# A new order for the output stage of the mixers: joined squares, groups C, D, A, B, pooled products between the rows

## The chip, the cores and the metric

The kernel runs on one core of a Trainium2 chip. The metric is the device time of one execution in microseconds. Five engines work side by side, each through its own list of instructions in its written order, and wait for each other by semaphores: TensorE (PE, its weight loads PEld), VectorE (DVE), ScalarE (ACT), GpSimd (POOL) and SyncE (SP), which issues the DMAs here.

## The reference

Two layers of a decoder trunk run over 320 tokens (256 of a prompt, 8 sequences of 8 samples) with 1024 channels, all in float32. Per layer:

```
x = LN(alpha*x + 0.5*(1+g1) * SwiGLU1(mod1(x)))
proj = mod2(x) @ W_in          -> u, v, xb, gate_b, gate_c, h, glu_a, glu_g
A = gelu(u) * (W_s (lower triangle, 4 heads of 64 channels) @ LN(gelu(v)) + b_s)
B = ((windowed mean of xb, windows 2/4/8/16) - xb) @ pool_w * pool_scale
C = gate_b * conv3(gate_c * h)
D = swish(LN(conv31(glu_a * sigmoid(glu_g)) + b))
x = LN(alpha*x + (1+g2) * (RMSnorm of each of A, B, C, D, 256 channels each) @ W_out)
x = LN(alpha*x + 0.5*(1+g3) * SwiGLU2(mod3(x)))
```

`mod(x) = x*(1+scale) + shift`, where scale, shift and the gates g are products of a conditioning vector with a matrix `w_ada` of 1024 x 9216 per layer. The last rows of the inputs of A, B, C and D are outputs too.

## The kernel before

Activations lie with 128 channels on the partitions and 320 tokens along the row, so 1024 channels are eight tiles and each group A to D is two. A weight tile is 128x128. For precision each weight unit (eight tiles, 128x1024) is split on the chip into a rounded high part (`whi`, a cast on ScalarE) and a low part (`wlo`, a subtraction on VectorE, L240), and each activation likewise; a product is then three matmuls of 320 columns.

All engines follow the order in which the program is written (`manual_schedule`); nothing is reordered. A class `Stream` loads raw weights through SyncE's queue six buffers ahead and splits one unit each time TensorE begins a new one (`next_unit`, called from `tile`): the cast and the subtraction stand in the lists of ScalarE and VectorE at that place. `ada_mm` puts in halves of the modulation product; each is four matmuls, one for each quarter of the 128 columns. When a part is done, `ada_step` takes it on by one stage at a time: a copy on ScalarE (`adev`, L485), a selection on TensorE (L489), an addition on VectorE (L498).

The mixers of a layer (`mix_body`) begin with ten windows of projections, during which VectorE works off 60 taps of D's convolution (L923). What then happens is written out by hand in `MIX_SEQ`, a list of words that `mix_body` performs one after the other:

- `mean`: the rest of the taps, then D's mean over 256 channels, two float32 matmuls with a constant matrix (L1116). `sub` takes it off.
- `sq g`, `stat g`, `pow g`, `bc g`, for a group g (4 is D's LayerNorm, 0 to 3 are the RMS norms of A to D): two squares on ScalarE (L834); their sum over the channels by matmuls with the squares as weights, for three blocks of tokens and both tiles (L541); a small addition on VectorE and a power on GpSimd (L1131, L1132); the broadcast over partitions by matmul (L611).
- `mul`, `hi`, `lo g`: the scaled product on VectorE (L842), its cast on ScalarE (L853), its low part on VectorE (L859).
- `vgain`, `sgu`, `sgate`: the gain of v, the spatial products of A (L1035, L1037), bias and gate on VectorE (L1046 to L1049).
- `pool0`, `pool1`: windowed sums of B's two tiles on VectorE (L958 to L969); `poolmm`: their two products on TensorE (L974), evicted on ScalarE (L977).
- `ko k`: the k-th of six rows of output products: for one of the first six input tiles, products into five accumulators (`kouter`, L681 to L686). `WO_GROUPS` says which group these tiles are of.

Behind the list comes the tail: a weight split, the next modulation's three products on VectorE, then the eight output tiles one by one (`WO_ORDER`) with the last two input tiles, each evicted (`evac`, L824 to L827), squared and added up for the next normalization, whose sums TensorE takes as `nbm` (L541).

Of the kernel before, what the change touches and what calls it, by code (L numbers as in the profile page):

```python
# [12 lines left out]
P = 128  # L13
# [52 lines left out]
WO_GROUPS = (2, 1, 3, 0)  # L66
# [4 lines left out]
    pool0 hc0 xb1 up0 val vstat up1 gc0 gb0 vnorm cconv0 gc1 hc1 gb1 mean cconv1 sub sq4 ada6 ctaps0 ctaps1 cgate0  # L71
    cgate1 stat4 pow4 vgain ada2 sq2 bc4 norm swish stat2 sq3 sgu pow2 pool1 ada2 stat3 bc2 pow3 poolmm mul2 hi2
    sq1 sgate bc3 lo2 sq0 ada2 stat1 mul3 hi3 pow1 ko0 stat0 lo3 pow0 bc1 mul1 ko1 hi1 lo1 step step bc0 mul0 hi0
    ada18 ko2 lo0 ko3 ko4 ko5
# [217 lines left out]
def sam(ap):  # L292
    return ap.rearrange("p (b t) -> p b t", t=NT_S)


class Kern:
# [568 lines left out]
    def mix_body(self, l, gb, G, late):  # L865
# [81 lines left out]
        def pool(j):  # L947
            e, es = eB[j], eBs[j]
            o = Y(f"pl{l}{j}")
            pl.append(o)  # L950
            sp = [mp.tile([P, 271], F32, tag="sp", bufs=2, name=f"s{i}p{l}{j}") for i in range(2)]
            ss = [mp.tile([P, NB, 23], F32, tag="ss", bufs=2, name=f"s{i}s{l}{j}") for i in range(2)]
            cp, cs_, sh = e, es, 1
            for g in range(2 * j + 2):
                np_, nss = sp[g % 2], ss[g % 2]
                lo = sh * 2 - 1
                p0 = 0 if g < 2 * j + 1 else 64
                V.tensor_tensor(np_[p0:P, lo:271], cp[p0:P, lo:271], cp[p0:P, lo - sh:271 - sh], op=ALU.add)  # L958
                V.tensor_tensor(nss[p0:P, :, lo:23], cs_[p0:P, :, lo:23], cs_[p0:P, :, lo - sh:23 - sh], op=ALU.add)
                if g // 2 == j:  # L960
                    q = slice(64 * (g % 2), 64 * (g % 2) + 64)
                    V.tensor_tensor(o[q, 0:16], np_[q, 15:31], self.inv[q, j, 0:16], op=ALU.mult)
                    V.scalar_tensor_tensor(o[q, 16:NP_], np_[q, 31:271], self.inv[q, j, 16:17], e[q, 31:271],
                                           op0=ALU.mult, op1=ALU.subtract)
                    V.scalar_tensor_tensor(sam(o[q, NP_:N]), nss[q, :, 15:23], self.inv[q, j, 16:17],
                                           es[q, :, 15:23], op0=ALU.mult, op1=ALU.subtract)
                cp, cs_ = np_, nss
                sh *= 2
            V.tensor_tensor(o[:, 0:16], o[:, 0:16], e[:, 15:31], op=ALU.subtract)  # L969

        def pool_mm():
            for jj in range(2):
                pb = self.mm(f"pb{l}{jj}")
# [54 lines left out]
        def spatial():  # L1028
            for jj in range(2):
                pt = self.mm(f"pm{l}{jj}")  # L1030
                for hh in range(2):
                    h = 2 * jj + hh
                    o = pt[64 * hh:64 * hh + 64]
                    for cc in range(2):
                        nc.tensor.matmul(o[:, cc * P:(cc + 1) * P], vb[cc][:, h * 64:(h + 1) * 64],  # L1035
                                         self.wsT[:, h, :], start=True, stop=True)
                    nc.tensor.matmul(o[:, NP_:N], vb[2][64:128, h * 64:(h + 1) * 64],  # L1037
                                     self.wsS[64:128, h, :], start=True, stop=True)
# [72 lines left out]
        def mean(_):  # L1111
# [3 lines left out]
            for j in range(2):  # L1115
                nc.tensor.matmul(rr[5][:, 0:N], self.o256, aD[j], start=(j == 0), stop=(j == 1))  # L1116
# [5 lines left out]
        def sq(grp):  # L1122
            qs[grp] = self.rms_sq(f"{l}{grp}", ys[grp])

# [45 lines left out]
        def taps_(n):  # L1170
            for _ in range(min(n, len(taps))):
# [6 lines left out]
               "norm": norm, "swish": swish, "ctaps": ctaps, "cgate": cgate, "vgain": lambda _: v_gain(),  # L1178
# [251 lines left out]
```

## Time and profile before

| | us |
|---|---|
| median of 3 runs | 1285.9 (1285.89 to 1292.28) |
| the profiled execution, its own time | 1289.18 |
| its span, first to last instruction | 1287.4 |
| output stage of layer 0, mean to last row | 350.96 to 387.68 |
| output stage of layer 1, mean to last row | 975.46 to 1013.66 |

The profile is one execution. Times in it count from its first instruction, and 1.8 us of the execution lie around the span. The stages are short against the whole, 36.7 and 38.2 us of 1287.4, and each holds some 280 matmuls of many kinds. Layer 0 and layer 1 run the same code; they differ in how many pieces of the modulation lie between the projections.

### The profile page before, as it was taken

How to read it: one execution, taken by the hardware profiler on the slowest of the kernel's cores; microseconds unless marked ns; L12 is line 12 of the kernel's file. 1: busy time of each engine (PE TensorE's matmuls, PEld its weight loads, DVE VectorE, ACT ScalarE, POOL GpSimd, SP SyncE). 2: the span in 40 equal slices, each digit the busy share in tenths (PEclk: the TensorE clock that was granted, in tenths of full speed). 3: DMA queues.
4: the chain of work that ended last, by engine and by line, in shares of the span. 5: the costliest groups of instructions: out<-in, count | busy, mean ns of one | idle time of the engine just before them, and what ended most of it. 6: DMA issues, size and time to landing. Idle time of an engine off the chain costs nothing.

```text
span 1287.4 us, 22297 instructions
## 1 busy us (share of the span) xinstructions
PE 1263.3 (98%) x9414; PEld 1213.7 (94%) x9414; DVE 730.0 (57%) x1321; ACT 555.8 (43%) x872; POOL 22.4 (2%) x39
## 2 busy tenths in 40 slices
PE   9999999999999999999999999999997999999996
PEld 8999999999888999999999999999995989999996
DVE  5644444468977644453575454445798775454444
ACT  3643333347444643343445343333653455343332
POOL 0000000000010000000000000000000000000000
PEclk9999999999999999999999999999998989999999
DMA  9865556568849854534465555454775694434301
GB/s 376 315 233 211 196 198 255 198 213 240 303 182 94 327 180 148 211 135 162 164 216 209 173 187 201 176 201 171 222 256 197 104 236 164 155 140 164 131 1 41
DMA packets 63748, 247.46 MB, mean 192 GB/s; under 512 B 31072, under 2 KB 33632, under 8 KB 34464
## 3 DMA queue, kind: packets, MB, share of 16 engines
q1 hardware_dynamic: 58912, 245.11, 56.9%
q8 instruction: 74, 1.21, 0.4%
q10 hardware_dynamic: 4736, 0.93, 0.4%
q14 instruction: 26, 0.21, 0.0%
HBM read 243.45 MB, written 2.57 MB: 191 GB/s over the span
## 4 chain that ended last, share of the span: by engine, by line
PE 90%; DVE 6%; ACT 2%; DMA 1%; issue 1%; POOL 0%; ACTq 0%; another core or an unknown queue 0%; SPq 0%; DVEq 0%
PE of L672 4%; PE adp L466 4%; PE oh L673 4%; PE of L673 4%; PE oh L674 4%; PE of L674 4%; PE oh L672 4%; PE uf L672 4%; PE uh L674 4%; PE uh L672 4%; PE uf L673 4%; PE uf L674 4%; PE uh L673 4%; PE gf L672 4%; PE gh L672 3%; PE gh L674 3%
## 5 line engine op out<-in xcount | busy, mean ns | idle before, releaser
L240 DVE TENSOR_TENSOR wlo<-raw,whi 128x1024 fp32r<-128x1024 f32 x312 | 373.1, 1223 | 137.3 <-ACT whi L232 136.4
L232 ACT CAST whi<-raw 128x1024 fp32r<-128x1024 f32 x312 | 315.3, 1045 | 24.4 <-issue 8.4
L672 PE MATMUL of<-hhf,whi 128*128 128x320 f32 x352 | 109.4, 311 | 0.0
L674 PE MATMUL of<-hhf,wlo 128*128 128x320 f32 x352 | 108.9, 310 | 0.0
L673 PE MATMUL of<-hlf,whi 128*128 128x320 f32 x352 | 108.9, 309 | 0.0
L672 PE MATMUL oh<-hhh,whi 128*128 128x320 f32 x352 | 108.5, 308 | 0.0
L674 PE MATMUL oh<-hhh,wlo 128*128 128x320 f32 x352 | 108.5, 308 | 0.0
L673 PE MATMUL oh<-hlh,whi 128*128 128x320 f32 x352 | 108.5, 308 | 0.0
L672 PE MATMUL uf<-xhif,whi 128*128 128x320 f32 x320 | 99.3, 310 | 0.0
L672 PE MATMUL uh<-xhih,whi 128*128 128x320 f32 x320 | 98.9, 309 | 0.0
L674 PE MATMUL uf<-xhif,wlo 128*128 128x320 f32 x320 | 98.8, 309 | 0.0
L673 PE MATMUL uf<-xlof,whi 128*128 128x320 f32 x320 | 98.8, 309 | 0.0
L673 PE MATMUL uh<-xloh,whi 128*128 128x320 f32 x320 | 98.8, 309 | 0.0
L674 PE MATMUL uh<-xhih,wlo 128*128 128x320 f32 x320 | 98.8, 309 | 0.0
L672 PE MATMUL gf<-xhif,whi 128*128 128x320 f32 x304 | 94.5, 311 | 0.0
L672 PE MATMUL gh<-xhih,whi 128*128 128x320 f32 x304 | 94.1, 309 | 0.0
L674 PE MATMUL gf<-xhif,wlo 128*128 128x320 f32 x304 | 93.9, 309 | 0.0
L673 PE MATMUL gf<-xlof,whi 128*128 128x320 f32 x304 | 93.9, 309 | 0.0
L674 PE MATMUL gh<-xhih,wlo 128*128 128x320 f32 x304 | 93.9, 309 | 0.0
L673 PE MATMUL gh<-xloh,whi 128*128 128x320 f32 x304 | 93.8, 309 | 0.0
L775 ACT CAST hhh<-sgh 128x320 fp32r<-128x320 f32 x44 | 20.2, 459 | 134.3 <-DVE sgh L772 133.8
L775 ACT CAST hhf<-sgf 128x320 fp32r<-128x320 f32 x44 | 20.2, 459 | 134.3 <-DVE sgf L772 134.3
(334 smaller groups left out, 2806.5 us busy)
## 6 DMA issues: line engine op xcount, KB each, us to landing
raw<-in_w_main SPq DMA_DIRECT2D x156, 1024.0 KB, 5.0
raw<-in_w_ada SPq DMA_DIRECT2D x72, 1024.0 KB, 6.8
out_yT<-x SPq DMA_DIRECT2D x8, 160.0 KB, 1.8
xt<-in_x SPq DMA_DIRECT2D x2, 512.0 KB, 4.2
wsT<-in_wsT SPq DMA_DIRECT2D x2, 256.0 KB
sgln<-in_sgln SPq DMA_DIRECT2D x2, 256.0 KB, 5.1
cD<-in_pre_d SPq DMA_DIRECT2D x4, 120.0 KB, 8.4
out_o_ds<-cD ACTq DMA_DIRECT2D x4, 120.0 KB, 9.7
```

The lines of the kernel that those rows point to most:

```text
L232: kk.nc.scalar.copy(hi, raw)
L240: self.kk.nc.vector.tensor_tensor(lo, raw, hi, op=ALU.subtract)
L466: nc.tensor.matmul(ps[32 * g:32 * g + 32, 0:w], self.cs[:, k, :], wt[:, h, g * w:(g + 1) * w], start=(k == 0), stop=(k == NK - 1))
L672: mm(ps, hi, xh, start=first, stop=False)
L673: mm(ps, hi, xl, start=False, stop=False)
L674: mm(ps, lo, xh, start=False, stop=last)
L775: nc.scalar.copy(hi, sg)
```

## The change

It rewrites the list, the order of the groups and four of the steps:

- `mean` adds D's two tiles on VectorE first and does one matmul instead of two. A new step `qa g` adds the two squares of a group on VectorE, so that `stat g` has three matmuls instead of six.
- The groups enter the output products in the order C, D, A, B (before: C, B, D, A). The weights of W_out are laid out in that order.
- C's broadcast stands ahead of D's group statistic, the spatial gate ahead of C's products, and C's power ahead of the spatial products.
- The 15 VectorE instructions of `pool1` are given out in three portions (`p4`, `p4`, `p9`) ahead of D's sum of squares, behind the first row of output products and behind the second; `poolmm` comes behind the third row, its second accumulator in the other PSUM tag.
- The spatial products alternate between two heads, which write to partitions 0 to 63 and 64 to 127.
- Three `step` words take the place of later `ada` words, which had nothing left to multiply and only called `ada_step`.

```diff
-WO_GROUPS = (2, 1, 3, 0)
+WO_GROUPS = (2, 3, 0, 1)
 MIX_SEQ = """
-    pool0 hc0 xb1 up0 val vstat up1 gc0 gb0 vnorm cconv0 gc1 hc1 gb1 mean cconv1 sub sq4 ada6 ctaps0 ctaps1 cgate0
-    cgate1 stat4 pow4 vgain ada2 sq2 bc4 norm swish stat2 sq3 sgu pow2 pool1 ada2 stat3 bc2 pow3 poolmm mul2 hi2
-    sq1 sgate bc3 lo2 sq0 ada2 stat1 mul3 hi3 pow1 ko0 stat0 lo3 pow0 bc1 mul1 ko1 hi1 lo1 step step bc0 mul0 hi0
-    ada18 ko2 lo0 ko3 ko4 ko5
+    pool0 hc0 xb1 up0 val vstat up1 gc0 gb0 vnorm cconv0 gc1 hc1 gb1 mean cconv1 sub sq4 ada6 ctaps0 qa4 ctaps1 cgate0
+    cgate1 stat4 pow4 vgain ada2 sq2 bc4 qa2 norm swish stat2 sq3 pow2 sgu p4 qa3 bc2 stat3 sgate sq0 mul2 hi2 pow3 step
+    qa0 step stat0 pow0 lo2 step bc3 mul3 hi3 ko0 p4 lo3 bc0 mul0 hi0 ko1 p9 lo0 ko2 poolmm ko3 sq1 qa1 stat1 pow1 ko4
+    bc1 mul1 hi1 ko5 lo1
 """.split()
...
-        def pool(j):
+        def pool_steps(j):
...
-                V.tensor_tensor(np_[p0:P, lo:271], cp[p0:P, lo:271], cp[p0:P, lo - sh:271 - sh], op=ALU.add)
+                yield V.tensor_tensor(np_[p0:P, lo:271], cp[p0:P, lo:271], cp[p0:P, lo - sh:271 - sh], op=ALU.add)
...
+        def pool_part(n):
+            if not pool1:
+                pool1.append(pool_steps(1))
+            for _ in range(n):
+                next(pool1[0], None)
 
         def pool_mm():
             for jj in range(2):
-                pb = self.mm(f"pb{l}{jj}")
+                pb = (self.rn if jj else self.mm)(f"pb{l}{jj}")[:, 0:N]
...
-                for hh in range(2):
-                    h = 2 * jj + hh
-                    o = pt[64 * hh:64 * hh + 64]
-                    for cc in range(2):
+                hs = [(2 * jj + hh, pt[64 * hh:64 * hh + 64]) for hh in range(2)]
+                for cc in range(2):
+                    for h, o in hs:
                         nc.tensor.matmul(o[:, cc * P:(cc + 1) * P], vb[cc][:, h * 64:(h + 1) * 64],
                                          self.wsT[:, h, :], start=True, stop=True)
+                for h, o in hs:
                     nc.tensor.matmul(o[:, NP_:N], vb[2][64:128, h * 64:(h + 1) * 64],
...
-            for j in range(2):
-                nc.tensor.matmul(rr[5][:, 0:N], self.o256, aD[j], start=(j == 0), stop=(j == 1))
+            s = mp.tile([P, N], F32, tag="rsq", bufs=4, name=f"sD{l}")
+            V.tensor_tensor(s, aD[0], aD[1], op=ALU.add)
+            nc.tensor.matmul(rr[5][:, 0:N], self.o256, s, start=True, stop=True)
...
+        def qa(grp):
+            a, b = qs[grp]
+            V.tensor_tensor(a, a, b, op=ALU.add)
+            qs[grp] = [a]
```

## Rows read from the trace of the kernel before

**Rows 1.** The page, part 1: busy time, share of the span, instructions per engine.
```profile
PE 1263.3 (98%) x9414; PEld 1213.7 (94%) x9414; DVE 730.0 (57%) x1321; ACT 555.8 (43%) x872; POOL 22.4 (2%) x39
```
**Rows 2.** Busy time by stretch: stage and tail of layer 0, before and in layer 1's.
```profile
core 0: us, PE busy (x) PEld busy (x) DVE busy (x) ACT busy (x) POOL busy (x), PEclk, DMA share, GB/s
350.96:387.68 36.72, 35.35 (x282) 31.23 (x281) 27.27 (x71) 17.23 (x32) 4.48 (x5) 0.95 0.49 183
387.68:405.92 18.24, 16.55 (x129) 15.54 (x127) 13.66 (x36) 8.54 (x18) 0.00 (x0) 1.00 1.04 105
969.60:975.46 5.86, 0.12 (x2) 0.00 (x1) 5.86 (x13) 0.42 (x1) 0.00 (x0) 0.93 0.43 158
975.46:1013.66 38.20, 36.83 (x280) 30.86 (x281) 27.40 (x71) 16.85 (x31) 4.48 (x5) 0.92 0.42 150
```
**Rows 3.** What TensorE waited for in the whole span: total us, times, longest us.
```profile
PE cmn L1116 <- DVE aD L923: 5.7, 1, 5.7
PE nbm L541 <- DVE Sm L583: 3.4, 2, 1.7
PE rr L541 <- ACT sqrm L834: 2.2, 2, 1.1
```
**Rows 4.** Instructions in order of time, layer 0, TensorE: start us, duration us, what.
```profile
350.96 1.24 PE L1116 MATMUL cmn<-aD,o 128*128 128x320 f32 x4
352.13 2.80 PE L466 MATMUL adp<-raw,cs 128*32 128x256 f32 x48
...
357.70 0.88 PE L611 MATMUL rr<-ident,rv 128*128 128x128 f32 x6 [0.29 <-POOL rv L1132]
358.41 1.50 PE L541 MATMUL rr<-o,sqrm 128*128 128x64 f32 x12
359.85 0.65 PE L1035 MATMUL pm<-wsT,v 128*64 128x128 f32 x4
...
363.19 0.64 PE L489 MATMUL adp<-sel,adev 128*128 128x36 f32 x4
```
**Rows 5.** The same for VectorE, layer 0.
```profile
349.93 1.22 DVE L240 TENSOR_TENSOR wlo<-raw,whi 128x1024 fp32r<-128x1024 f32 x1
...
355.40 0.89 DVE L1091 TENSOR_TENSOR yC<-yC,gbs 128x320 f32<-128x320 f32 x2
...
360.03 0.43 DVE L958 TENSOR_TENSOR s0p<-eb 128x270 f32<-128x270 f32 x1
...
363.78 0.17 DVE L969 TENSOR_TENSOR pl<-pl,eb 128x16 f32<-128x16 f32 x1
...
366.89 0.42 DVE L1046 TENSOR_TENSOR yA<-pm,sgb 128x256 f32<-128x256 f32 x1
...
368.87 0.89 DVE L859 TENSOR_TENSOR ml<-yC,mh 128x320 fp32r<-128x320 f32 x2
...
369.82 1.00 DVE L842 SCALAR_TENSOR_TENSOR aD<-aD,par,rr 128x320 f32<-128x320 f32 x2
...
372.29 1.23 DVE L240 TENSOR_TENSOR wlo<-raw,whi 128x1024 fp32r<-128x1024 f32 x1 [1.40 <-ACT whi L232]
```
**Rows 6.** The same for ScalarE, layer 0.
```profile
361.03 0.35 ACT L485 COPY adev<-adp 128x256 f32<-128x256 f32 x1
...
371.21 1.99 ACT L232 CAST whi<-raw 128x1024 fp32r<-128x1024 f32 x2
```
**Rows 7.** The same for TensorE, layer 1.
```profile
975.46 2.50 PE L1116 MATMUL cmn<-aD,o 128*128 128x320 f32 x4 [5.74 <-DVE aD L923]
977.89 4.54 PE L466 MATMUL adp<-raw,cs 128*32 128x256 f32 x48
...
997.70 0.40 PE L681 MATMUL wo<-mh,whi 128*128 128x320 f32 x1
...
999.98 1.45 PE L541 MATMUL rr<-o,sqrm 128*128 128x64 f32 x12
```
**Rows 8.** VectorE at the first eviction of the tail, layer 0.
```profile
388.76 0.23 DVE L824 TENSOR_TENSOR evsm<-wo,ada 128x64 f32<-128x64 f32 x1 [0.36 <-PE wo L674]
```

More of the change, by code (lines that the diff above doesn't have):

```diff
@@ L957, in pool @@
                 p0 = 0 if g < 2 * j + 1 else 64
-                V.tensor_tensor(np_[p0:P, lo:271], cp[p0:P, lo:271], cp[p0:P, lo - sh:271 - sh], op=ALU.add)
-                V.tensor_tensor(nss[p0:P, :, lo:23], cs_[p0:P, :, lo:23], cs_[p0:P, :, lo - sh:23 - sh], op=ALU.add)
+                yield V.tensor_tensor(np_[p0:P, lo:271], cp[p0:P, lo:271], cp[p0:P, lo - sh:271 - sh], op=ALU.add)
+                yield V.tensor_tensor(nss[p0:P, :, lo:23], cs_[p0:P, :, lo:23], cs_[p0:P, :, lo - sh:23 - sh], op=ALU.add)
                 if g // 2 == j:
                     q = slice(64 * (g % 2), 64 * (g % 2) + 64)
[L962 to L966, printed above, removed]
+                    yield V.tensor_tensor(o[q, 0:16], np_[q, 15:31], self.inv[q, j, 0:16], op=ALU.mult)
+                    yield V.scalar_tensor_tensor(o[q, 16:NP_], np_[q, 31:271], self.inv[q, j, 16:17], e[q, 31:271],
+                                                 op0=ALU.mult, op1=ALU.subtract)
+                    yield V.scalar_tensor_tensor(sam(o[q, NP_:N]), nss[q, :, 15:23], self.inv[q, j, 16:17],
+                                                 es[q, :, 15:23], op0=ALU.mult, op1=ALU.subtract)
                 cp, cs_ = np_, nss
                 sh *= 2
-            V.tensor_tensor(o[:, 0:16], o[:, 0:16], e[:, 15:31], op=ALU.subtract)
+            yield V.tensor_tensor(o[:, 0:16], o[:, 0:16], e[:, 15:31], op=ALU.subtract)
+        def pool(j):
+            for _ in pool_steps(j):
+                pass
+        pool1 = []
+        def pool_part(n):
[3 more added lines that the diff above has]
+                next(pool1[0], None)
         def pool_mm():
             for jj in range(2):
-                pb = self.mm(f"pb{l}{jj}")
+                pb = (self.rn if jj else self.mm)(f"pb{l}{jj}")[:, 0:N]
                 nc.tensor.matmul(pb, self.pw[:, jj, :], pl[jj], start=True, stop=True)
@@ L1177, in mix_body @@
                "vnorm": lambda _: v_norm(), "cconv": cconv, "t": taps_, "mean": mean, "sub": sub, "sq": sq, "stat": stat, "pow": pw_, "bc": bc, "mul": mul, "hi": hi, "lo": lo,
-               "norm": norm, "swish": swish, "ctaps": ctaps, "cgate": cgate, "vgain": lambda _: v_gain(),
+               "norm": norm, "swish": swish, "ctaps": ctaps, "qa": qa, "p": pool_part, "cgate": cgate, "vgain": lambda _: v_gain(),
                "pool": pool, "poolmm": lambda _: pool_mm(), "sgu": lambda _: spatial(),
```

## The prediction, made before the changed kernel ran

> **What bounds the kernel now.** I read the page's busy times first, then the stretches around the two output stages, then what TensorE waited for there, then each engine's instructions in order of time. TensorE is busy 98% of the span, VectorE 57% [rows 1]: time saved on TensorE counts, unless another engine is late. In the two stretches that the change rewrites (36.7 us in layer 0, 38.2 us in layer 1) VectorE is busy 27.3 of 36.7 us, far above its share of the whole, and ScalarE 17.2 [rows 2]. TensorE's waits there are small, 1.1 us a layer for squares and 0.3 for D's power [rows 3, 4]; the large one, 5.7 us in layer 1, stands ahead of the stage, where the D taps on VectorE end after the last projection [rows 3]. In the tail behind the stage TensorE ends first and waits 1.7 us a layer for VectorE's sums [rows 3]: the evictions run as one chain over VectorE and ScalarE, so what delays the first eviction delays the layer.
>
> **Prices.** A pitch is start to next start. On TensorE: the mean 1.17 us, a statistic of 12 records 1.44 (358.41 to 359.85), a broadcast 0.71, the spatial products 3.34 (359.85 to 363.19), one sixth of the modulation run 0.46 [rows 4]; a row of output products 2.28 (997.70 to 999.98, [rows 7]). On VectorE: two 128x320 products 0.89, so 0.40 pitch and 0.49 to the end for one; two scaled products 1.00; the spatial gate 1.98 (366.89 to 368.87); the pooled products 3.8 for 15 instructions (360.03 to 363.78, and the last); a weight split 1.14 pitch [rows 5]. On ScalarE: a weight cast 1.0, the modulation copy 0.35 [rows 6]. Each engine works in its written order, so I laid the new order down engine by engine: an instruction starts when its engine is free and its last operand is there, plus 0.03 us from engine to engine (the rounded gap in rows like 371.21 and 372.29). Laid down the same way, the old order ends layer 0's tail 0.12 us late and layer 1's 0.75 us late against the trace; I take these off.
>
> **What is removed.** Ten statistics lose half their records (0.72 each, 3.6 a layer), two means lose half (0.58 each). The spatial products now alternate between the two halves of the columns. No row of before shows two halves side by side: the bounds are no gain (3.34 stays) and, by the modulation run, full overlap. There 24 products of 256 columns take 2.80 us, 0.12 each, where the four 320-column records of the mean take 1.17: four column groups overlap about four times [rows 4]. Two groups would give half, 1.67. I take 1.8, nearer to the row; no gain would cost 0.46 a layer at the end, since part of it lies beside VectorE. In all some 5.7 us of TensorE per layer go.
>
> **What is added.** Six sums on VectorE per layer, 0.40 each, 2.4 us, and each stands between ScalarE's squares (or the taps) and TensorE.
>
> **Layer 0, step by step.** Mean: taps and a weight split occupy VectorE to 351.06 [rows 5], the new sum ends 351.55, the half mean ends 352.20, as before: gain nothing. D's LayerNorm statistic ends 0.6 earlier, but its power instruction stands on VectorE behind the taps and gates of C, now 0.4 longer: its broadcast comes at 357.8, before 357.70 [rows 4], and TensorE idles 1.2. C's statistic waits for its sum, which stands ahead of D's normalization: 359.2 instead of 358.4, and D's normalization is 0.4 later. The spatial products end at 361.7, 1.5 ahead of before, then C's broadcast and D's group statistic end at 363.1. Now VectorE has, from 360.2: four pool steps 1.2, D's sum (it waits for swish and squares to 361.6) 0.4, the gate 1.98, C's products 0.92, a power, A's sum 0.4: 365.4. ScalarE can cast C only behind those products, and the modulation copy stands behind that cast; TensorE waits for it 2.65 us, to 365.7 (A's statistic would wait to 365.4 anyway). Output products of C start at 367.6, 2.6 ahead of before (370.18). But VectorE's road to the pooled products is long: D's products end 369.1; D's cast and the weight cast on ScalarE end at 370.6, while VectorE waits 1.6 for the split (1.40 before, [rows 5]); split, four pool steps, D's low parts, A's products (1.14, 1.06, 0.80, 0.92) to 374.5; A's cast and the next weight cast, again 1.6 of waiting; split to 377.2; the last seven pool steps 1.7: 378.97. TensorE is done with the first three rows and the first pooled product at 375.6 and waits 3.4 us for the second, with two rows of output products (ko3 to ko5), B's statistic and broadcast queued behind it. From there TensorE needs ko3, 1.1 of waiting for B's sum (behind eviction, weight cast and squares), ko4, the broadcast, ko5: 388.9, where before it was 387.68 [rows 2]. That is +1.2. The tail's first eviction is later still: B's low parts end 388.8, and behind them stand a weight split that waits for its cast and the three modulation products; it starts at 391.0, before 388.76 [rows 8], +2.3. The tail's chain carries it to the next normalization: 408.04 - 405.92 - 0.12 = +2.0 us.
>
> **Layer 1.** The mean starts 0.8 later (the sum behind the last tap, 976.3 for 975.46) and is half as long at the low clock, so it ends 0.4 earlier, 977.5 for 977.9 [rows 7]. VectorE is ahead here, so D's halved LayerNorm statistic counts: its broadcast is 0.8 earlier. From there the steps are those of layer 0: the replay ends at 1034.67 against 1031.90, less 0.75: +2.0.
>
> **Clock.** In the old stage the granted clock averages 0.95 in layer 0, 3.7 us at the lower of its levels (1.2 GHz), after waits of 0.3 and 1.1 us; in layer 1 it is 0.92, about 6 us, after the wait of 5.7 [rows 2 to 4]; the same modulation run then takes 4.54 us instead of 2.80 [rows 4, 7]. The new waits (1.2, 0.8, 2.65, 3.4, 1.1) are more and longer. Four us at the lower level from the second pooled product on add only 0.5 per layer, since VectorE is the later one there; another 3.5 us of it from A's statistic on bring this to 1.3. I take 1.0 per layer, bounds 0 and 2.5 (the latter if a row such as ko4 or ko5 falls in it too). The Trainium skill (TensorE: Matmul & The Clock Gate, section on psum-queue depth-cycling) speaks against this change: frequent short idles between groups of matmuls let the clock swing between its levels. By that rule the low stretches last through the stage, which is the second rival below.
>
> **What moves at no cost.** DMAs: the weight loads follow VectorE's splits, one to two us later than before, while the DMA share of the stage is 0.49 [rows 2]; without that slack a split would wait. POOL's five powers keep their number. The new order of groups only renames the weight tiles. A's statistic and B's take their accumulator from C's and A's products, which end before either is due.
>
> **Sum.** +2.0 +2.0 +2x1.0 = +6.0 on the profiled 1289.18 (span 1287.4): 1295.2. That execution lies 3.3 us above the median, 1285.9, which I take to shift alike: 1292.0, with 1288 to 1297 for this case.
>
> **Rivals.** *Pooled products in time* (faster): if VectorE reaches the last pool steps 3.4 us earlier, the wait at the second pooled product goes, the tail starts at 385.5 and each layer gains 1.4: 1285.9 - 2.8 = 1283; with every cut of TensorE effective 11.4 less, 1274.5. For it: TensorE is 98% busy. Against: VectorE's chain is made of instructions whose durations stand in the rows, and its two waits for a weight cast are there already in the old order. It decides from the point where pool's end lies before 375.6 in layer 0. *Clock low through the stage*: 4.54/2.80 is 1.6 times; with bounds of 2.5 per layer and no overlap of the spatial products (0.46) it is 1285.9 + 4.0 + 5.9 = 1296, to 1299. For it the many waits; against it that the same 1.1 us wait ahead of the first row of output products leaves that row at full clock in layer 1, 2.28 us [rows 3, 7]. *Waits and cuts cancel*: VectorE's additions hide in its old idle (9.4 us of 36.7, [rows 2]) and the stage ends as before: 1286 to 1288. For it the idle; against it that this idle is waiting on ScalarE and TensorE within the same chain.
>
> **Chances.** Forecast 0.62, pooled products in time 0.12, clock 0.14, cancel 0.12. 0.5% is 6.4 us, about what a measurement of this kernel can tell from no change. The forecast is split about evenly by that bound: slower 0.31 + 0.14 + 0.02 = 0.47, faster 0.10, the rest 0.43. Range 1281 to 1299: down over half of the faster case, up over the clock case.
>
> **What would show it.** In the changed profile: TensorE waits about 3.4 us on a pool instruction at the second pooled product and about 2.6 us at the modulation's selection, in both layers; statistics of 6 records at 0.7 pitch; spatial products 1.7 to 1.8 together; output products starting about 2.6 us earlier in the stage and their fourth row later than before. A pool end before TensorE's third row, or a stage shorter than 36.7 us, would make the forecast wrong.

## The result and the profile after

The changed kernel takes 1301.55 us (median of 6 runs, 1298.21 to 1303.57) against 1288.66 us for the kernel before, run beside it (1285.89 to 1294.05, 6 runs). The ratio is 1.0087, 95% interval [1.0065, 1.0109]: slower, as forecast, but by 11 us (by the ratio) to 13 us (by the medians) where the forecast had 6. The time lies above the range. Of the 9.5 us between it and the forecast of 1292.0, 2.8 are the base: the forecast started from 1285.9, the median of three runs, and with six runs that is 1288.66.

The profiled execution of the changed kernel took 1301.87 us, its span is 1300.1. Busy time of each engine in the span, as in [rows 1]:

```profile
PE 1262.2 (97%) x9350; PEld 1212.7 (93%) x9350; DVE 735.6 (57%) x1333; ACT 556.5 (43%) x872; POOL 27.1 (2%) x39
```
TensorE does 1.1 us less, VectorE 5.6 us more, the span (1287.4 before) is 12.7 us longer. GpSimd does as many instructions as before and is busy 4.7 us longer with them; that is the first sign of what the forecast missed. The stretches that answer to [rows 2], stage and tail of layer 0 and of layer 1:

```profile
core 0: us, PE busy (x) PEld busy (x) DVE busy (x) ACT busy (x) POOL busy (x), PEclk, DMA share, GB/s
351.68:393.30 41.62, 34.75 (x248) 30.07 (x249) 28.11 (x74) 16.69 (x31) 7.83 (x5) 0.84 0.45 173
393.30:412.62 19.32, 16.60 (x129) 15.58 (x127) 14.65 (x37) 8.97 (x19) 0.00 (x0) 0.99 0.71 74
984.10:1024.75 40.65, 34.32 (x249) 28.43 (x249) 27.95 (x74) 16.66 (x31) 5.76 (x5) 0.86 0.41 152
1024.75:1044.04 19.29, 16.56 (x129) 15.54 (x127) 14.62 (x36) 8.95 (x19) 0.00 (x0) 0.99 0.93 74
```
The stages are 41.6 and 40.7 us long, before 36.7 and 38.2 [rows 2]. TensorE is busy for less of them, its granted clock is 0.84 and 0.86 (0.95 and 0.92), and the five powers take 7.83 us of GpSimd in layer 0. What TensorE waited for in the whole span (total us, times, longest), as in [rows 3]:

```profile
PE cmn L1129 <- DVE sD L1128: 7.2, 2, 6.7
PE nbm L541 <- DVE Sm L583: 5.5, 2, 2.7
PE pb L986 <- DVE pl L969: 3.9, 2, 2.0
PE rr L611 <- POOL rv L1150: 3.5, 2, 3.2
PE adp L489 <- ACT adev L485: 3.1, 2, 2.5
PE rr L541 <- DVE sqrm L1140: 2.7, 3, 1.1
```
The forecast's waits are there: the second pooled product (`pb`), the selection (`adp`), the sums of squares. One is there that it had at 1.2 us and that is 3.2: D's broadcast in layer 0, released by GpSimd. TensorE in layer 0, in order of time:

```profile
351.68 0.81 PE L1129 MATMUL cmn<-sD,o 128*128 128x320 f32 x2 [0.49 <-DVE sD L1128]
...
360.23 0.88 PE L611 MATMUL rr<-ident,rv 128*128 128x128 f32 x6 [3.20 <-POOL rv L1150]
360.94 1.43 PE L541 MATMUL rr<-o,sqrm 128*128 128x64 f32 x6
362.30 1.12 PE L1046 MATMUL pm<-wsT,v 128*64 128x128 f32 x8
...
365.23 1.54 PE L611 MATMUL rr<-ident,rv 128*128 128x128 f32 x6
366.56 1.49 PE L541 MATMUL rr<-o,sqrm 128*128 128x64 f32 x6
368.62 1.07 PE L489 MATMUL adp<-sel,adev 128*128 128x36 f32 x4 [0.58 <-ACT adev L485]
```
The broadcast right behind the wait still takes 0.88 us, as at the full clock [rows 4]; the next one, at 365.23, takes 1.54. The granted clock is at the lower level, 1.2 GHz, from 361.0 to 374.6. GpSimd's power that TensorE waited for:

```profile
357.13 3.04 POOL L1150 TENSOR_TENSOR rv<-rv,mhalf 128x3 f32<-128x3 f32 x1 [27.03 <-DVE rv L1149]
```
and in the kernel before the same instruction, on three numbers per partition:

```profile
356.68 0.96 POOL L1132 TENSOR_TENSOR rv<-rv,mhalf 128x3 f32<-128x3 f32 x1 [26.66 <-DVE rv L1131]
```
There VectorE had waited 0.15 us ahead of the small addition that hands the power its operand:

```profile
356.44 0.16 DVE L1131 TENSOR_SCALAR rv<-rr 128x3 f32<-128x3 f32 x1 [0.15 <-PE rr L541]
```
VectorE beside it, in the changed kernel: the small addition, reached without a wait, then v's gain and C's joined squares without a gap, to 359.46.

```profile
356.90 0.15 DVE L1149 TENSOR_SCALAR rv<-rr 128x3 f32<-128x3 f32 x1
356.98 2.09 DVE L1034 TENSOR_TENSOR v<-v,sgln 128x256 f32<-128x256 f32 x6
358.98 0.48 DVE L1140 TENSOR_TENSOR sqrm<-sqrm,sqrm 128x320 f32<-128x320 f32 x1
```
The power ends 0.71 us behind that run. In layer 1 the same instructions stand beside it, but there VectorE had waited 0.82 us ahead of the small addition, and the power took 0.96 us:

```profile
990.85 0.16 DVE L1149 TENSOR_SCALAR rv<-rr 128x3 f32<-128x3 f32 x1 [0.82 <-PE rr L541]
```
So in layer 1 the forecast's steps show undisturbed (TensorE):

```profile
984.10 1.43 PE L1129 MATMUL cmn<-sD,o 128*128 128x320 f32 x2 [6.73 <-DVE sD L1128]
...
994.29 0.66 PE L1046 MATMUL pm<-wsT,v 128*64 128x128 f32 x8
...
995.99 0.88 PE L611 MATMUL rr<-ident,rv 128*128 128x128 f32 x6
996.71 0.83 PE L541 MATMUL rr<-o,sqrm 128*128 128x64 f32 x6
...
1000.02 1.07 PE L489 MATMUL adp<-sel,adev 128*128 128x36 f32 x4 [2.48 <-ACT adev L485]
```
The spatial products take 1.70 us together (994.29 to 995.99; forecast 1.7 to 1.8, before 3.34), the selection waits 2.48 (forecast 2.65), and behind that wait the clock is again low. Last, the sums of the next normalization in layer 0:

```profile
412.62 1.54 PE L541 MATMUL nbm<-o,Sm 128*128 128x64 f32 x6 [2.72 <-DVE Sm L583]
413.95 1.49 PE L541 MATMUL rbm<-o,Qm 128*128 128x64 f32 x6
415.23 1.49 PE L611 MATMUL nbm<-ident,vm 128*128 128x128 f32 x6
```
The wait is 1.0 us longer than before [rows 3], and what follows runs at 1.2 GHz; before, the first of these took 0.88.

### The profile page after: what moved, and what is told of

The parts are those of the page before. It is cut to its first block, busy times and chain, and to the rows that moved or that the text cites. A ratio compares the mean times of both kernels' runs of the same rounds, so it can differ in the third digit from the quotient of the medians.

```text
span 1300.1 us, 22179 instructions
## 1 busy us (share of the span) xinstructions
PE 1262.2 (97%) x9350; PEld 1212.7 (93%) x9350; DVE 735.6 (57%) x1333; ACT 556.5 (43%) x872; POOL 27.1 (2%) x39
## 4 chain that ended last, share of the span: by engine, by line
PE 68%; issue 19%; DVE 9%; ACT 2%; POOL 0%; POOLq 0%; ACTq 0%; DVEq 0%
PE of L672 4%; PE of L673 4%; PE of L674 4%; PE uf L672 4%; PE adp L466 4%; PE uf L674 4%; PE uf L673 4%; PE gf L672 3%; PE gf L674 3%; PE gf L673 3%; DVE wlo L240 3%; DVE aD L923 3%; PE oh L674 2%; PE oh L673 2%; PE oh L672 2%
```

## The experiments

Besides these two, seventeen kernels were run. For each, "layer 0" and "layer 1" are the time in us from the start of D's mean to the start of the normalization's sums in its profile (behind added matmuls, where there are some), the ratio is that of its runs to those of the kernel before beside it, with its interval. Where the text says that a kernel is so many us faster or slower, that is its ratio taken of 1290 us.

| kernel | ratio | layer 0 | layer 1 |
|---|---|---|---|
| before | 1 | 54.96 | 56.44 |
| changed | 1.0087 [1.0065, 1.0109] | 60.94 | 59.94 |
| inter_only | 0.9962 [0.9939, 0.9986] | 51.79 | 53.70 |
| join_only | 1.0053 [1.0033, 1.0072] | 61.38 | 56.76 |
| order_nojoin | 1.0057 [1.0034, 1.0080] | 59.46 | 59.49 |
| fill | 1.0077 [1.0050, 1.0104] | 59.00 | 59.41 |
| vgain_late | 1.0092 [1.0065, 1.0118] | 60.59 | 62.08 |
| pool_8 | 1.0046 [1.0026, 1.0066] | 60.25 | 58.11 |
| step_early | 1.0069 [1.0043, 1.0095] | 60.09 | 59.24 |
| qa4_only | 1.0074 [1.0043, 1.0106] | 61.46 | 55.33 |
| qa4_fill | 1.0051 [1.0026, 1.0076] | 55.27 | 55.12 |
| order_fill | 1.0052 [1.0033, 1.0071] | 58.49 | 59.37 |
| order_mended | 0.9992 [0.9974, 1.0011] | 53.79 | 56.48 |
| nbm_fill | 1.0080 [1.0052, 1.0107] | 61.59 | 59.69 |
| fill_all | 1.0069 [1.0044, 1.0095] | 59.16 | 59.23 |
| best3 | 0.9933 [0.9910, 0.9956] | 52.20 | 50.58 |
| best_all | 0.9934 [0.9916, 0.9953] | 51.01 | 53.61 |
| best_c | 0.9910 [0.9895, 0.9925] | 49.79 | 52.14 |
| best_c_fill | 0.9889 [0.9868, 0.9909] | 49.80 | 50.06 |

The two right columns come from one execution each, and the low clock does not last equally long in every one. The edit of *nbm_fill* stands behind layer 0's stage and tail, and yet its layer 0 is 0.65 us longer than the changed kernel's: the clock is low for 17.1 us there instead of 13.7. So a difference of about a microsecond between two rows is weak evidence.

**One part at a time.** *inter_only*: the kernel before with the alternating spatial products.

```diff
-                for hh in range(2):
...
+                for cc in range(2):
+                    for h, o in hs:
```


> Kernel before, with only the spatial products alternating between the two column halves. Overlap theory: the four heads' products take about 1.7 us instead of 3.34, and since TensorE is the late engine there, each layer's next normalization comes 1.6 us earlier: about 3 us faster in all (ratio 0.9975). Rival (vector chain): the products are shorter, but VectorE's pooled products set what follows, and nothing is gained (ratio 1.000).

Measured 1286.48 us, 4.9 faster. The products overlap. Each layer is 3 us shorter, more than the 1.6 saved; the clock is at 1.00 behind the first 20 us of both (0.96 in layer 0 before).

*join_only*: the old order with joined squares and mean.

```diff
-... ctaps0 ctaps1 cgate0 cgate1 stat4 ...
+... ctaps0 qa4 ctaps1 cgate0 cgate1 stat4 ...     (and so for groups 2, 3, 1, 0, and the mean)
```


> Kernel before, old order of groups and pooled products whole, with the joined mean and joined squares alone (the sums put where the changed kernel has them, as far as the old order allows). Written-order theory: statistics of 6 records at 0.8 us, but TensorE then waits for the sums on VectorE: layer 0 up to 1.0 us later, layer 1 within 0.3, ratio 1.000 to 1.001. Rival (TensorE bound): 3.6 us of statistics and 0.6 of mean per layer come off, ratio 0.994.

Measured 1296.56 us, 6.8 slower: both theories missed. The power takes 3.04 us in layer 0, TensorE waits 3.2 for it; layer 0 is 6.4 us longer, with the clock low for 20.5 us, layer 1 0.3.

*order_nojoin*: the changed kernel without any join (the mean is two matmuls again, too).

```diff
-            V.tensor_tensor(a, a, b, op=ALU.add)
-            qs[grp] = [a]
+            pass
```

> The changed kernel without the joined squares and the joined mean: new order of groups, split pooled products and alternating spatial products stay. Written-order theory: most of the loss is the order's, about 2.9 us per layer plus the low clock behind its waits, ratio 1.005 to 1.007; the second pooled product still waits 2 to 3.4 us. Port theory (GpSimd's first power is held up by VectorE's uninterrupted run in layer 0): without the added sum VectorE is idle ahead of that power, which takes 1.0 us instead of 3.04. Rival (the sums are the loss): ratio 1.000 or below.

Measured 1297.53 us, 7.4 slower. The power takes 0.96 us. TensorE waits 3.4 us (layer 0) and 1.9 us for the second pooled product. So the written order loses most of the changed kernel's 11 us without any join, and the joins bring the long power. The order's share is larger than it looks: this kernel holds the alternating products, which alone gain 4.9 us, so that against *inter_only* the order costs some 12 us. The parts don't add up: 12 less 4.9 and the 6.8 of the joins would be 14, and the changed kernel loses 11.

**The clock.** *fill*: the changed kernel with matmuls of constants in two of TensorE's waits.

```diff
+            for _ in range(n):
+                nc.tensor.matmul(ps, self.o256, self.o256, start=True, stop=True)
...
-... sq2 bc4 ... stat3 sgate ...
+... sq2 f13 bc4 ... stat3 f9 sgate ...
```


> The changed kernel with idle matmuls (their result is not used) in two of TensorE's waits: 13 ahead of D's broadcast in layer 0, 9 ahead of the modulation's selection in both layers. Clock theory: the granted clock of the stages rises from 0.84 and 0.86 to over 0.95, and 3 to 5 us of the loss go (ratio to before about 1.005). Written-order theory: the clock rises, but VectorE's and ScalarE's chain sets the end of the stage and under 1.5 us are gained (ratio 1.008).

Measured 1300.24 us, ratio 0.0010 lower than the changed kernel's: the written-order theory. The clock is up in the first 20 us of layer 0 (1.00 for 0.73), and the wait at the second pooled product grows to 3.4 us in both layers, as the forecast had it. Most of what is saved ahead is waited for there. Selection and second pooled product of layer 0:

```profile
367.89 0.64 PE L486 MATMUL adp<-sel,adev 128*128 128x36 f32 x4 [0.65 <-ACT adev L482]
...
381.19 0.91 PE L983 MATMUL pb<-pl,pw 128*128 128x320 f32 x2 [3.43 <-DVE pl L966]
```

*qa4_only* and *qa4_fill*: the kernel before with one added instruction per layer, the sum of D's squares; the second also with 11 matmuls of constants ahead of D's broadcast in layer 0.

```diff
-... ada6 ctaps0 ctaps1 ... sq2 bc4 ...
+... ada6 ctaps0 qa4 ctaps1 ... sq2 f11 bc4 ...
```


> The kernel before with one addition: D's two squares are added on VectorE in the midst of C's taps, and D's statistic has 6 records. By the replay without a lock: +0.2 us in layer 0, -0.65 in layer 1, so no change to be measured. Theory A (D's power is shut out where VectorE reaches its operand without having waited, so that its run is unbroken): the power takes about 2.5 us in layer 0, until v's gain ends, TensorE waits for it 1.5 us or more longer than before, the clock falls there and the whole is 1.5 to 4 us slower than the kernel before. Theory B (C's joined squares behind v's gain made the run too long, or it hangs on something else of the change): the power takes 0.96 us and the time is that of before within 1 us.

> The kernel with D's joined squares alone, and 11 matmuls of constants in layer 0 in the place where TensorE waits 2.8 us for D's power; they add nothing to the outputs. It parts what the shut-out power costs by itself from what the granted clock behind it costs. Theory A (clock): the power still takes about 2.6 us, but the granted clock stays at 1.0 in the 14 us behind it; from D's mean to the next normalization's sums layer 0 takes 2 us more than before (56.9 us) instead of 6.5 more (61.5), so the whole is 4 us faster than with the joined squares alone. Rival (the wait itself, and the order behind it, are the loss): the clock is up and layer 0 still takes over 60 us.

The power takes 2.64 us in layer 0 of both, beside v's gain alone. The first 20 us of layer 0 and the rest, without the matmuls of constants:

```profile
352.88:372.88 20.00, 17.20 (x131) 12.70 (x129) 12.04 (x41) 6.31 (x13) 3.62 (x2) 0.74 0.69 263
372.88:414.34 41.46, 38.68 (x273) 36.91 (x272) 29.30 (x66) 19.49 (x37) 2.55 (x3) 0.96 0.49 81
```
and with them:

```profile
352.73:372.73 20.00, 18.77 (x175) 14.52 (x173) 15.29 (x51) 8.93 (x20) 4.46 (x3) 1.00 0.69 263
372.73:408.00 35.27, 33.58 (x250) 32.56 (x251) 25.86 (x57) 16.83 (x31) 1.70 (x2) 1.00 0.58 95
```
The clock column goes from 0.74 to 1.00 and the layer from 61.46 to 55.27 us, with the same shut-out power: in this kernel the low clock behind one wait of 2.8 us costs 6.2 us. What the wait costs by itself isn't parted: with it layer 0 is 0.3 us longer than before, but its clock is at 1.00 throughout, where before it was low for 3.4 us, and its first statistic is shorter. The runs of both kernels spread widely (1293.97 to 1306.86; 1287.44 to 1303.80, three of 12 at 1288). *qa4_only* is 9.5 us slower than before where 1.5 to 4 were expected, and the whole times part the two kernels by 1.1 us only (by the medians; 3 by the ratios, whose intervals overlap). The profile of *qa4_fill* is of one of its three fast runs: the profiles show the mechanism, not how often it strikes.

*order_fill*: the new order without joins, with 13 and 7 matmuls of constants ahead of the second pooled product.

```diff
+                if jj:
+                    ps = self.mm(f"fill{l}", 128)
+                    for _ in range(7 if l else 13):
+                        nc.tensor.matmul(ps, self.o256, self.o256, start=True, stop=True)
```


> The new order without the joins, and matmuls of constants (13 in layer 0, 7 in layer 1) ahead of the second pooled product, where TensorE waits 3.4 and 1.9 us. Theory A (half of what the new order loses is the low clock behind its waits): the granted clock stays at 1.0 from there on in layer 0 (0.50 to 0.53 for 7 us without them), layer 0 takes 56.7 us from mean to sums instead of 59.5, layer 1 about 1 us less, in all -3 to -4 us on the new order without joins. Rival (VectorE's chain sets the end there, so TensorE's clock is beside the point): under 1 us.

The clock is at 1.00 behind it, layer 0 is 1.0 us shorter than without them and layer 1 0.1, and the ratio is 0.0005 lower. The rival, that VectorE's chain sets the end there, is nearer.

*nbm_fill*: the changed kernel with 11 of them ahead of the normalization's sums.

```diff
+        if nm.startswith("m"):
+            for _ in range(11):
+                nc.tensor.matmul(nt[:, 0:P], self.o256, self.o256, start=True, stop=True)
         S = self.stat(nt, [self.accS], self.o1024)
```

> The changed kernel with 11 matmuls of constants ahead of the sums for the normalization behind the mixers, in both layers, where TensorE now waits 2.7 us for VectorE's last sum (1.7 before); they add nothing to the outputs. Theory A (the longer wait there lets the granted clock fall, and the normalization's own matmuls then run at the lower level: 8.4 us from the sums to the next projection instead of 6.9): sums, broadcasts and the modulation run take their times at 2.4 GHz, the stretch from sums to next projection becomes 6 to 7 us, and the whole is 2 to 4 us faster than the changed kernel. Rival (VectorE and ScalarE set the pace of the normalization): under 1 us, the saved time comes back as a wait for the casts.

From the sums to the next projection it takes 7.18 and 5.92 us (8.38 and 8.41 without them); the sums of layer 0 themselves start 0.65 us later behind the mean. The ratio of the whole can't be told from that of the changed kernel: the stretch shows it, the time is inconclusive.

*fill_all*: the edits of *fill* and *nbm_fill* together, and that of *order_fill* with 13 in both layers.

> The changed kernel with matmuls of constants in all five waits that its stage and tail have (13 ahead of D's broadcast in layer 0, 9 ahead of the modulation's selection, 13 ahead of the second pooled product, 11 ahead of the normalization's sums). Theory A (the part of the miss that the forecast did not hold is the granted clock): with the clock up the waits of the written order are left alone, and the time comes to the forecast's sum without its clock term: +4 us on the kernel before, ratio 1.003, some 7 us under the changed kernel. Theory B (the order's waits are larger than forecast even at the full clock): ratio 1.006 or more, and the stage of layer 0 still takes over 58 us from mean to sums (55.0 before, forecast 57).

Both layers, mean to sums:

```profile
352.26:411.42 59.16, 56.36 (x467) 50.79 (x467) 42.37 (x110) 25.50 (x49) 7.83 (x5) 1.00 0.61 146
981.35:1040.58 59.23, 56.00 (x440) 48.65 (x440) 42.47 (x110) 25.50 (x49) 5.75 (x5) 0.95 0.56 128
```
Theory B: at a clock of 1.00 layer 0 still takes 59.16 us, 4.2 more than before. The waits alone are more than the forecast's sum. Some 0.4 us a layer of it may be the added matmuls' own: the second pooled product starts 29.9 us behind layer 0's mean, 29.4 in *fill*, which has none ahead of it.

**The order's waits.** *pool_8* and *step_early*: the changed kernel with the last nine pooled steps beside the second four; or with the modulation's copy behind the spatial products.

```diff
-... ko0 p4 lo3 bc0 mul0 hi0 ko1 p9 lo0 ...
+... ko0 p13 lo3 bc0 mul0 hi0 ko1 lo0 ...
-... sgu p4 ... pow3 step qa0 step ...
+... sgu step p4 ... pow3 step qa0 ...
```


> The changed kernel with the last nine pooled steps brought forward to stand with the second four, behind the first row of output products (13 in one place). Theory A (the written order costs its time at the second pooled product, which waits for VectorE's last steps, and at what stands behind it): that wait of 2.0 us a layer goes, a smaller one of 0.6 us appears at the third row of output products and B's statistic waits 2.3 instead of 1.1 us; by the replay -1.5 us a layer, -3 us on the changed kernel. Rival (the waits are only where the loss shows, and VectorE's whole work ahead of the tail sets its end): the wait moves and the time stays within 1 us.

> The changed kernel with the modulation's copy on ScalarE brought forward from behind C's weight cast to behind the spatial products. Theory A (the selection's wait of 2.5 us in layer 1 is real loss): the wait moves to A's statistic, where it is 1.8 us by the replay; -0.76 us in layer 1 and, since TensorE is late there already, 0 to -0.76 in layer 0: -1 us on the changed kernel. Rival (the low granted clock behind the wait is what costs): the clock of the stretch stays low because the wait only moves, and the time stays within 0.5 us.

With *pool_8* 1295.87 us, ratio 0.0041 lower than the changed kernel's, some 5 us (expected 3); its wait is gone, and the two layers of its profile are 0.7 and 1.8 us shorter. With *step_early* 1299.24 us, some 2 us (expected 1), inside the interval; the selection's wait is gone, and in layer 1 it has moved to A's statistic (1.85 us, expected 1.8; joined squares take 3.4 us of waiting there).

*order_mended*: both edits, without joins.

> The new order without the joins, with the last nine pooled steps put to the second four and the modulation's copy brought forward to behind the spatial products: both large waits of the new order mended. Theory A (these two waits, with the clock they take along, are what the new order loses): layer 0 takes 55 us from mean to sums and layer 1 56.5, as before, TensorE's waits at the second pooled product and at the selection go, and the time is that of the kernel before, ratio 0.998 to 1.002, some 8 us under the new order without joins. Rival (groups C, D, A, B in this order lose by themselves, since VectorE has more to do ahead of the tail): two thirds of the 7 us stay, ratio 1.004.

```profile
351.39:405.18 53.79, 49.38 (x409) 44.07 (x407) 40.65 (x106) 25.68 (x50) 5.57 (x5) 1.00 0.66 160
976.69:1033.17 56.48, 52.09 (x406) 45.09 (x406) 40.87 (x106) 25.29 (x49) 5.58 (x5) 0.95 0.57 137
```
Layer 0 and layer 1 take 53.8 and 56.5 us (55.0 and 56.4 before), the time is that of before: theory A, and the places of two words made the loss of *order_nojoin*, with the clock that they took along. It doesn't show that the rest of the order is free. This kernel too holds the alternating products; against *inter_only* its layers are 2.0 and 2.8 us longer and its ratio is 0.0030 higher (the intervals overlap). That the groups can stand in this order without such a loss, *best3* below shows.

**When the power is shut out.** *vgain_late*: the changed kernel with v's gain behind D's normalization.

```diff
-... pow4 vgain ada2 sq2 bc4 qa2 norm swish ...
+... pow4 ada2 sq2 bc4 norm qa2 vgain swish ...
```


> The changed kernel with v's gain put behind D's normalization (and behind C's joined squares): VectorE has nothing to do while D's power runs. Theory A (the power of 3.04 us in layer 0 is GpSimd shut out by VectorE's unbroken run beside it): the power takes 0.85 us in both layers, TensorE waits about 1.1 us for it in layer 0 instead of 3.2 and keeps its higher clock there; against that v's gain now stands 2 us later, ahead of the spatial products, which the replay without any lock prices at +1.5 us a layer: layer 0 about as long as in the changed kernel, layer 1 +1.5, in all 0 to +2 us on the changed kernel. Theory B (the long power comes from something else, such as the instruction itself or its operands' tiles): it stays at 3 us in layer 0, and the whole is 3 us or more slower than the changed kernel.

GpSimd in layer 0:

```profile
357.04 0.85 POOL L1147 TENSOR_TENSOR rv<-rv,mhalf 128x3 f32<-128x3 f32 x1 [27.03 <-DVE rv L1146]
362.31 2.21 POOL L1147 TENSOR_TENSOR rv<-rv,mhalf 128x3 f32<-128x3 f32 x1 [4.42 <-DVE rv L1146]
```
D's power takes 0.85 us with VectorE idle, and TensorE waits 1.0 us for it: theory A. But C's power, whose small addition VectorE now reaches without a wait, takes 2.21 us beside pooled steps and a sum, in both layers, which neither theory had. The whole takes 1302.21 us, 0.7 us above the changed kernel, as expected.

*best3*, *best_all*: the list written anew; the second with matmuls of constants ahead of D's broadcast (7, layer 0), D's mean (22, layer 1) and the sums (6).

```diff
-... mean cconv1 ... stat4 pow4 vgain ada2 sq2 bc4 qa2 norm ...
+... mean vgain cconv1 sub ctaps0 ada6 ctaps1 sq4 cgate0 stat4 sgu pow4 cgate1 sq2 bc4 p4 qa2 norm ...
+... hi2 lo2 stat0 step p4 bc3 ko0 mul3 pow0 hi3 p9 lo3 ko1 poolmm bc0 sq1 ko2 ...
```


> A list written anew from what the runs showed: groups C, D, A, B and alternating spatial products as in the changed kernel, v's gain right behind D's mean, so that nothing unbroken runs on VectorE beside D's power, joins only where VectorE has room (C, A and B; not D's squares nor its mean), the last nine pooled steps ahead of the second row of output products, the modulation's copy early. By the replay, which knows neither the clock nor a power that is shut out, the longest wait in the stage is 0.42 us and each layer is 4.4 (layer 0) and 5.0 us (layer 1) shorter than before: -9 us, ratio 0.993. Rival (TensorE's idle time elsewhere or the clock takes it back, as it did with half of the alternating products' gain): the ratio of the alternating products alone, 0.996.

> The newly written list (1280.7 us in its run) with matmuls of constants in TensorE's waits: 7 ahead of D's broadcast in layer 0 (wait 1.9 us), 22 ahead of D's mean in layer 1 (5.8 us) and 6 ahead of the normalization's sums behind the mixers (1.7 us, both layers). Theory A (the low clock behind these waits is time): the modulation run behind the mean in layer 1 takes 2.8 us instead of 4.5, layer 0 about 51 instead of 52.2 us from mean to sums, the normalizations 1 us less each; -3 to -5 us, ratio 0.990. Rival: the list alone, 0.993, since what is gained there is waited for on VectorE and ScalarE.

*best3* takes 1280.69 us, ratio as expected, though in layer 0 the power was shut out once more (2.61 us, a wait of 1.9), which the list was written to prevent. *best_all* gains nothing more: with the mean's clock up, D's statistic in layer 1 is ready before VectorE comes to it, and the power that took 1.03 us there takes 2.62:

```profile
977.60 2.62 POOL L1158 TENSOR_TENSOR rv<-rv,mhalf 128x3 f32<-128x3 f32 x1 [30.69 <-DVE rv L1157]
```
*best_c*, *best_c_fill*: both with C's second taps (products with a scalar) beside the power in place of C's gate, pooled steps and a sum.

```diff
-... ctaps0 ada6 ctaps1 sq4 cgate0 stat4 sgu pow4 cgate1 sq2 bc4 p4 qa2 ...
+... ctaps0 ada6 sq4 cgate0 stat4 p2 sgu pow4 ctaps1 cgate1 sq2 bc4 p2 qa2 ...
```


> The newly written list (1280.7 us) with D's power put ahead of the second half of C's taps (and two of the first four pooled steps ahead of it), so that what VectorE runs beside the power are products with a scalar instead of a run of sums and products of two tiles. Theory A (the power is shut out by a run of two-tile instructions that VectorE enters without a wait): the power takes 0.85 to 0.97 us in both layers (2.61 in layer 0 of that list), TensorE's wait of 1.9 us for it goes, the clock stays at 1.0, and layer 0 takes 50.5 us from mean to sums instead of 52.2: -1 to -2 us. Theory B (any VectorE work beside it shuts it out): the power again takes over 2 us and the time is that of the list before.

> The same with the matmuls of constants ahead of D's mean in layer 1 and ahead of the normalization's sums. There the power was shut out in layer 1 too, once TensorE's higher clock had D's statistic ready earlier. Theory A: with the power beside C's taps it takes under 1 us in both layers, layer 1 takes 49 us from mean (behind the added matmuls) to sums instead of 53.6, and the whole is 3 to 6 us under the list with these matmuls: 1275 us, ratio 0.989. Theory B: the power is over 2 us in both layers, 1280 us.

The power takes 1.02 us in all four layers, though in three of them VectorE came to its small addition without a wait: theory A. Layer 0 of *best_c* is 2.4 us shorter than that of *best3*. Its layer 1 is 1.6 us longer, with a short power in both; the low clock reaches further there, so that the modulation run behind the mean takes 4.09 us instead of 3.10. In layer 1 of *best_c_fill*:

```profile
976.95 1.02 POOL L1158 TENSOR_TENSOR rv<-rv,mhalf 128x3 f32<-128x3 f32 x1 [30.23 <-DVE rv L1157]
```
*best_c* takes 1278.45 us, 23 us under the changed kernel, and *best_c_fill* 1276.49 us, 14 under the kernel before: groups C, D, A, B, alternating products and three of the six sums, with other places for a few words, and in the second with matmuls of constants.

## Why the prediction was wrong, point by point

The direction and the places of the order's waits were right; the size failed in the steps below. The account, from the profiled executions, of the span's 12.7 us. The forecast's two +2.0 hold the later start of the mean, so the layers are counted here from the last projection:

| | forecast | measured | how split |
|---|---|---|---|
| layer 0, last projection to sums | 2.0 and clock 1.0 | 6.63 | ahead of the mean 0.65, waits 4.20 (fill_all less before), clock 1.78 (changed less fill_all) |
| layer 1, last projection to sums | 2.0 and clock 1.0 | 4.49 | ahead of the mean 0.99, waits 2.79, clock 0.71 |
| sums to next projection | 0 | 1.45 and -0.14 | clock behind a longer wait |
| the rest of the span | 0 | 0.3 | places without an edit |

The split into waits and clock is as good as one profile of each kernel allows, and the waits hold the 0.4 us of *fill_all*'s own matmuls.

**"POOL's five powers keep their number": the step that failed.** Their number stayed and their price did not. I left the price of before (0.85 to 0.97 us) and never asked on what it hangs. In layer 0 the joined sum of D's squares made VectorE late enough to come to the power's operand without a wait, and the power took 3.04 us; TensorE waited 3.20 where I had 1.2. *qa4_only* shows that one such sum is enough. The delay stays to the end: counted from the end of the mean, D's broadcast comes 2.2 us later than forecast (7.8 for 5.6), and with the clock kept up, in *fill*, the selection (15.4 for 13.5) and the second pooled product (28.7 for 26.8) are still 1.9 late. That is most of what layer 0's waits have above the forecast. The Trainium skill (SBUF — State Buffer, "two separate sides") says that a GpSimd instruction that reads SBUF and a VectorE instruction with two inputs in SBUF exclude each other, and that the later one waits for the whole other instruction. It was the rule that spoke against this change, and I weighed another. The trace agrees with its kind and goes beyond its size: 3.04 us are not one instruction but a run of seven. That the two share a port is the page's; the trace shows only that the power ends behind VectorE's run.

**"Less 0.75".** My replay of layer 1 gave +2.77, the mean's later start among it, and I took off what it had missed in the old order. Measured at the clock of before (0.95 from mean to sums in both, *fill_all*) it is 0.97 ahead of the mean and 2.79 behind it, 3.8 in all. The replay was short by up to 1.0 even as it stood, and the deduction made it 1.8; which step of the replay was short stays open. A replay's miss in one order is no correction for another.

**"I take 1.0 per layer".** With 1.78 and 0.71 the sum is near the forecast's 2.0, but not its reason: the clock fell behind D's power in layer 0 and in the selection's wait in layer 1, not from the second pooled product on, so the near sum is luck. In the changed kernel a low clock of 14 us costs 1.8, in *qa4_only* 6.2: I read this as full cost where TensorE sets the end, and little where VectorE's chain is later anyway. The Trainium skill (TensorE: Matmul & The Clock Gate, "psum-queue depth-cycling") says that frequent short idles between groups of matmuls let the clock swing between its levels and cost throughput. The trace agrees that it is low for longer: 13.7 of the 41.6 us of layer 0's stage, before 3.4 of 36.7, though in one piece. My second rival, low through the whole stage, did not come; it is nearer to layer 0 than my stretch of 4 us.

**The tail's chain ends at the sums.** I stopped my sum there. The wait ahead of them grew from 1.7 to 2.7 us, and the normalization behind, which begins at 1.2 GHz in both layers, took 1.45 us more in layer 0. *nbm_fill* gives 1.2 and 2.5 us of these stretches back.

**What held.** The joined mean gains nothing: it waits 6.7 us in layer 1 where two matmuls waited 5.7. Spatial products at 1.70 (1.67 was my bound for full overlap of two column groups). Six records of statistics at 0.8, 0.1 above the forecast. The selection's wait 2.48 (2.65) in layer 1; in layer 0, where TensorE comes late at the low clock, it is 0.6. The wait for the pooled steps is 2.0, and 3.4 as forecast in *fill*, where the clock is up ahead of it. *Waits and cuts cancel* fell; *pooled products in time* fell for the changed kernel, and *best3* shows that it could be had with the same groups.

What stays open: the spread of the runs with joined squares of D alone, the miss of layer 1's replay, and what ends a long power. The small rest of the span is luck: stretches with no edit differ among all these kernels by more (from the first normalization's end to layer 1's mean 561.9 to 567.0 us).

## What to carry to other kernels

A small instruction on GpSimd that TensorE waits for is priced by what VectorE does beside it: in this case it was short where VectorE waited, read PSUM or multiplied by a scalar. Look for its longest duration in the trace, not its mean. When a change makes a wait on TensorE, price the matmuls behind it at the lower clock until a row shows it up again, and ask which engine is then the later one: that decides whether the clock costs all of it or little. Where many VectorE instructions stand between TensorE's needs, the place of each counts more than the work saved: the same order of groups gave 1301.55 us and, with three of the six sums and other places, 1278.45 (*best_c*).

## What the runs showed of the hardware that was not expected

- The power of three numbers takes 0.85 us with VectorE idle. Beside VectorE instructions on SBUF alone it ended 0.70 to 0.74 us behind the end of one of them, in every row looked at: of the first one (0.96 to 1.03 us, 1.76 to 1.80 beside a weight split), or of a whole run of sums and products of two tiles (2.21, 2.61 to 2.64, 3.04). In all the long ones VectorE had reached the small addition ahead of the power without a wait; yet not all such were long (0.85 where an instruction with an operand in PSUM followed, 1.02 to 1.03 where a product with a scalar or C's low parts did, and 0.97 to 0.98 beside the same pooled steps in *join_only*, *fill* and *fill_all*, layer 0). What lets it in is not shown.
- The granted clock, once at 1.2 GHz behind a wait of about 3 us with short broadcasts and statistics to do, stayed there for 13.7 us (changed kernel, *qa4_only* and *step_early*, layer 0), 17.1 us (*pool_8*, *nbm_fill*) and 20.5 us (*join_only*). Behind the second pooled product, with rows of output products to do, it was low for 3 to 7 us in layer 0 of *order_nojoin* (a wait of 3.4 us) and of *vgain_late* (2.4) and in both layers of *fill* (3.4); in both layers of the changed kernel (2.0) it did not fall.
- Matmuls of constants keep it up: 11 of them, 2.6 us in a wait of 2.8, brought the 20 us from D's mean on from 0.74 to 1.00 (*qa4_only* and *qa4_fill*).
